# The RWKV-7 outputs of a hybrid two-layer model: one 64x64 inverse per chunk, outputs of two chunks beside the second solve, and low parts on GpSimd

## The chip, the cores and the metric

The kernel runs on one core of a Trainium2 chip. The metric is the time of one launch on the device, in microseconds (us); less is better. TensorE (PE in the rows) multiplies, VectorE (DVE), ScalarE (ACT) and GpSimd (POOL) do elementwise work, and SyncE (SP) issues the transfers.

## The reference

512 tokens of width 1024 pass two layers in float32. Layer 0 mixes with RWKV-7 (8 heads of 64) and gated linear attention (GLA, 4 heads), layer 1 with differential attention; a SwiGLU block of hidden width 2816 follows each. The change touches the mixer of layer 0 alone. Its RWKV part runs, for each head, over the tokens

```
def step(S, inp):
    r_t, w_t, k_t, v_t, a_t, b_t = inp
    sa = einsum('bhvk,bhk->bhv', S, a_t)
    S = S * w_t[:, :, None, :] + sa[..., None] * b_t[:, :, None, :] + v_t[..., None] * k_t[:, :, None, :]
    return S, einsum('bhvk,bhk->bhv', S, r_t)
...
y = rwkv7_recurrence(rh, heads(decay), kh, vh, -kk, kk * heads(a))
y = ((y - mean) * rsqrt(var + 64e-5)).reshape(Bsz, T, 512) * ln_w + ln_b
bonus = sum(rh * kh * r_k, axis=-1, keepdims=True) * vh
o_a = (y + bonus) * g                    # g = sigmoid(xg @ g1) @ g2
o_b = rms(gla(...)) * gla_norm * silu(gg)
return concatenate([o_a, o_b], axis=-1) @ w_out
```

## The kernel before

The matrices are transposed: channels lie on the 128 partitions, the 512 tokens along the free dimension. A projection (`form_a`) splits each weight block in a high part (`whi`, ScalarE, L96) and a low part (`wlo`, VectorE, L97) and issues three fast matmuls per 128x128 block (`mm3`, L107 to L109); other products are plain float32, and the trace shows two matmul records for each of them.

The recurrence runs in blocks of 64 tokens. A chunk `c` here is 128 channels, that is two heads, with all 8 blocks of tokens; there are four. `Chunk` makes the inputs of one (`key`, `receptance`, `value`) and the Gram products (`gram`): per head and block a unit lower triangular 64x64 matrix whose inverse is needed. `solve` inverts its 32x32 diagonal blocks for two chunks at once: 31 steps of a multiplication (`tmp`, L633) and an addition (`xl`, L635), framed by 32x32 transposes (L624, L638). The first solve (chunks 0, 1) runs on GpSimd during chunks 2 and 3, the second (chunks 2, 3) on VectorE.

`rwkv_out` forms a chunk's output. It applies the 64x64 inverse by three rounds of 128x128 products: the diagonal inverse (`z`, L661), the block below the diagonal (L668, added on VectorE as `w`, L670) and the diagonal inverse again (L675). Then come the state products (L697, L709), six state steps in series (L718, L719), the read-out (L728, L734), the group norm (L744 to L759), the bonus (L760) and the output gate (product L753 and L754, factor L761). A generator yields between the stages, and `interleave(gens, 5)` writes the four chunks with a lag of five stages.

The order on each engine comes from a planner: it places every instruction by the written order and modelled times, and the hardware keeps that order. `gla_gates` (24 matmuls for each of four heads, `gg`) is written ahead of the second solve and uses the first set of PSUM banks; the outputs use the second set, which takes the same banks. Behind the outputs the output projection runs in two halves: GLA's (`part`, into `pd` banks) and RWKV's (`ohi`, `olo`, into `o` banks).

Of the kernel before, what the change touches and what calls it, by code (L numbers as in the profile page):

```python
# [16 lines left out]
P = 128  # L17
T = 512
# [428 lines left out]

def gla_gates(g, pool, ob):
    nc = g.nc
    for h in range(4):  # L450
        pg = dbank(g)
        form_a(g, pg, g.ap["win"][16 + h], g.xhi, g.xlo)
        gg = pool.tile([P, T], F32, name="gg", bufs=2)
        nc.vector.tensor_mul(gg, pg, g.rstd)
        nc.scalar.activation(gg, gg, AF.Silu)
        o = pool.tile([P, T], F32, name="o", bufs=2)
        nc.sync.dma_start(o, ob[h])
        nc.gpsimd.tensor_mul(o, o, gg)
        nc.sync.dma_start(ob[h], o)


class Chunk:
# [74 lines left out]
    def receptance(self):  # L537
# [7 lines left out]
        nc.vector.scalar_tensor_tensor(q4(r), q4(r), self.col("rw_r_k"), self.k, op0=ALU.mult, op1=ALU.mult)  # L545
        self.pbn = bank(g)
        nc.tensor.matmul(self.pbn, lhsT=m0.bones, rhs=r, start=True, stop=True)

    def value(self):
# [5 lines left out]
        for e in range(2):  # L555
            nc.vector.scalar_tensor_tensor(self.vs[:, :, 1 - e], qe(p)[:, :, e], self.col("mu_v"), qe(d)[:, :, e],
                                           op0=ALU.mult, op1=ALU.add)
        for e in range(2):
            nc.vector.tensor_mul(qe(d)[:, :, e], qe(self.pbn)[:, :, e], self.vs[:, :, 1 - e])
        nc.sync.dma_start(st.bon[c], d)  # L560

    def gram(self):
        g, m0, st, c = self.g, self.m0, self.st, self.c
        nc, ar, bk = g.nc, self.ar, self.bk
        for e in range(2):
# [49 lines left out]
def solve(g, st, sp, eng, cs):  # L615
# [3 lines left out]
    n = cs[0]  # L619
    xl = sp.tile([P, 32, 32], F32, name=f"xl{n}")  # L620
    nc.gpsimd.memset(xl, 0.0)
    nc.gpsimd.memset(xl.rearrange("p t i -> p (t i)")[:, 0::33], 1.0)
    al = sp.tile([P, 32, 32], F32, name=f"al{n}")
    nc.vector.transpose(al.rearrange("p t i -> p (t i)"), st.dg.rearrange("p a c i t -> p t (a c i)"))  # L624
# [3 lines left out]
    buf = sp.tile([P, 256], F32, name=f"tmp{n}")  # L628
    yield
    for s in range(31):  # L630
# [4 lines left out]
        eng.tensor_add(xl[:, s + 1:, 0:s + 1], xl[:, s + 1:, 0:s + 1], tmp)  # L635
    yield
# [10 lines left out]
def rwkv_out(g, m0, st, sp, c, zeros):  # L647
# [3 lines left out]
    no, G = zeros[c % 2]  # L651
    for e in range(2):
        rows = slice(64 * e, 64 * e + 32)
        nc.scalar.copy(no.rearrange("p (a i) x -> p a i x", a=2)[rows, :, :, 64 * e + 32:64 * e + 64],
                       st.n21[rows, :, c])
    x4 = lambda t: t.rearrange("p (u x) -> p u x", u=4)
    z, w = {}, {}
    for ih in range(2):
        pu = x4(bank(g, use))
        for i in range(4):  # L660
            nc.tensor.matmul(pu[:, i], lhsT=st.xd[:, ih, c, i], rhs=st.r[:, ih, c, i], start=True, stop=True)  # L661
        z[ih] = sp.tile([P, 4, P], F32, name="z", bufs=2)
        nc.scalar.copy(z[ih], pu)
    yield
    for ih in range(2):
        pw = x4(bank(g, use))
        for i in range(4):
            nc.tensor.matmul(pw[:, i], lhsT=no[:, 4 * ih + i], rhs=z[ih][:, i], start=True, stop=True)  # L668
        w[ih] = sp.tile([P, 4, P], F32, name="w", bufs=2)
        nc.vector.tensor_add(w[ih], pw, st.r[:, ih, c])  # L670
    yield
    for ih in range(2):
        pu = x4(bank(g, use))
        for i in range(4):
            nc.tensor.matmul(pu[:, i], lhsT=st.xd[:, ih, c, i], rhs=w[ih][:, i], start=True, stop=True)  # L675
# [636 lines left out]
```

## Time and profile before

| | |
|---|---|
| median of 3 runs | 1336.83 us (1335.76 to 1337.07) |
| profiled execution | 1336.43 us, its span 1334.6 us |
| TensorE busy | 1302.7 us, 98% of the span |
| VectorE, ScalarE, GpSimd busy | 701.3, 563.9, 216.3 us |
| mean granted TensorE clock | 0.992 |

The span is the profiled part of the execution; the 1.8 us between it and its time lie around it. Busy time counts an engine as busy while any of its instructions runs; matmuls overlap, so a row's mean duration is longer than the distance to the next one. The granted clock is a share of 2.4 GHz.

### The profile page before, as it was taken

The numbers are of one execution on the slowest core, as the hardware profiler recorded it, in microseconds if no ns is written. First come the engines' busy times: TensorE is split into PE (matmuls) and PEld (weight loads), VectorE is DVE, ScalarE is ACT, GpSimd is POOL, SyncE is SP. The second block draws the span as 40 slices with busy tenths as digits, with TensorE's granted clock in tenths as the row PEclk, the third lists the DMA queues.
The fourth block names the chain that finished last, engine by engine and source line by source line (L and its number), as shares of the span: only waits on it lengthen the run. The fifth ranks groups of instructions, "written<-read, shape, count | busy, mean of one in ns | idle before, by whom it ended". The sixth has DMA issues, their size and how long they took to land.

```text
span 1334.6 us, 17753 instructions
## 1 busy us (share of the span) xinstructions
PE 1302.7 (98%) x6856; PEld 1065.9 (80%) x6856; DVE 701.3 (53%) x1197; ACT 563.9 (42%) x957; POOL 216.3 (16%) x205
## 2 busy tenths in 40 slices
PE   8999989899999999999999999999999999999998
PEld 6788767687878888888888887887888888888886
DVE  7465778954554433334434258888643434433342
ACT  5555866353443222223334347777432322322232
POOL 3011084211511110011112001110201110011110
PEclk9999989899999999999999999999999999999999
DMA  6222222423645323433234332211333323553331
GB/s 196 66 64 87 72 72 87 156 72 108 233 140 163 95 77 97 115 104 99 75 88 125 96 95 64 52 46 46 110 102 102 93 75 97 148 127 98 101 100 63
DMA packets 52719, 133.72 MB, mean 100 GB/s; under 512 B 6067, under 2 KB 8499, under 8 KB 52636
## 3 DMA queue, kind: packets, MB, share of 16 engines
q1 hardware_dynamic: 51772, 131.43, 32.8%
q8 instruction: 54, 0.88, 0.3%
q10 hardware_dynamic: 864, 1.17, 0.2%
q14 instruction: 29, 0.24, 0.1%
HBM read 121.74 MB, written 11.36 MB: 100 GB/s over the span
## 4 chain that ended last, share of the span: by engine, by line
PE 90%; DVE 7%; ACT 2%; issue 1%; DMA 0%; DVEq 0%; ACTq 0%
PE pd L109 24%; PE pd L108 24%; PE pd L107 24%; PE po L1054 2%; DVE wlo L97 1%; DVE tmp L633 1%; DVE xl L635 1%; PE sc L1029 1%; PE sc L1030 1%; PE o L109 1%; PE o L108 1%; PE o L107 1%; PE pt L1050 0%; PE o L675 0%; PE po L108 0%
## 5 line engine op out<-in xcount | busy, mean ns | idle before, releaser
L96 ACT CAST whi<-wraw 128x1024 fp32r<-128x1024 f32 (+2 forms) x240 | 210.4, 879 | 521.1 <-PE pd L108 302.0
L109 PE MATMUL pd<-xhi,wlo 128*128 128x512 f32 x1032 | 406.6, 394 | 0.0
L107 PE MATMUL pd<-xhi,whi 128*128 128x512 f32 x1032 | 405.6, 393 | 0.9 <-ACT xhi L188 0.9
L108 PE MATMUL pd<-xlo,whi 128*128 128x512 f32 x1032 | 405.8, 393 | 0.0
L97 DVE TENSOR_TENSOR wlo<-wraw,whi 128x1024 fp32r<-128x1024 f32 (+2 forms) x240 | 252.4, 1054 | 137.1 <-ACT whi L96 136.2
L107 PEld LDWEIGHTS pd<-xhi,whi 128*128 128x128 f32 x1032 | 193.8, 188 | 42.1 <-ACT xhi L188 1.3
L108 PEld LDWEIGHTS pd<-xlo,whi 128*128 128x128 f32 x1032 | 193.8, 188 | 41.1 <-issue 0.2
L109 PEld LDWEIGHTS pd<-xhi,wlo 128*128 128x128 f32 x1032 | 193.9, 188 | 40.4
L231 POOL TENSOR_TENSOR hlo<-h,hhi 128x512 fp32r<-128x512 f32 x44 | 67.3, 1529 | 546.3 <-ACT hhi L230 546.3
L227 DVE TENSOR_TENSOR ut<-pd,rstd 128x512 f32<-128x512 f32 x44 | 30.4, 692 | 146.3 <-PE pd L109 146.3
L107 PE MATMUL pd<-hhi,whi 128*128 128x512 f32 x264 | 102.7, 389 | 0.0
L108 PE MATMUL pd<-hlo,whi 128*128 128x512 f32 x264 | 102.7, 389 | 0.0
L109 PE MATMUL pd<-hhi,wlo 128*128 128x512 f32 x264 | 102.7, 389 | 0.0
L224 DVE TENSOR_TENSOR gt<-pd,rstd 128x512 f32<-128x512 f32 x44 | 30.4, 692 | 123.5 <-PE pd L109 121.4
L108 PEld LDWEIGHTS pd<-hlo,whi 128*128 128x128 f32 x264 | 49.6, 188 | 10.3
L107 PEld LDWEIGHTS pd<-hhi,whi 128*128 128x128 f32 x264 | 49.5, 188 | 10.3
L109 PEld LDWEIGHTS pd<-hhi,wlo 128*128 128x128 f32 x264 | 49.5, 188 | 10.3
L1034 ACT ACTIVATE s<-s,mn 128x384 f32<-128x384 f32 (+3 forms) x64 | 35.7, 559 | 21.4 <-DVE mn L1031 20.8
L230 ACT CAST hhi<-h 128x512 fp32r<-128x512 f32 x44 | 27.4, 622 | 35.5 <-DVE h L229 35.5
L240 DVE TENSOR_TENSOR xT<-pd,xT 128x512 f32<-128x512 f32 x24 | 16.6, 692 | 46.2 <-PE pd L109 46.2
L1010 POOL TENSOR_TENSOR qst<-q,qst 64x512 fp32r<-64x512 f32 x8 | 13.2, 1646 | 167.9 <-DVE qst L1008 167.9
L157 POOL TENSOR_TENSOR ssum<-nsq,ssum 128x512 f32<-128x512 f32 x21 | 31.5, 1498 | 49.9 <-ACT nsq L153 49.4
(384 smaller groups left out, 1837.4 us busy)
## 6 DMA issues: line engine op xcount, KB each, us to landing
wraw<-in_gate SPq DMA_DIRECT2D x44, 512.0 KB, 3.7
wraw<-in_up SPq DMA_DIRECT2D x44, 512.0 KB, 3.6
wraw<-in_win SPq DMA_DIRECT2D x40, 256.0 KB, 2.7
wraw<-in_down SPq DMA_DIRECT2D x24, 384.0 KB, 3.1
wraw<-in_wqk SPq DMA_DIRECT2D x16, 512.0 KB, 3.6
wraw<-in_down SPq DMA_DIRECT2D x24, 320.0 KB, 2.8
wraw<-in_downt SPq DMA_DIRECT2D x10, 512.0 KB, 3.7
xT<-in_xT SPq DMA_DIRECT2D x16, 256.0 KB, 3.9
```

Source lines behind the costliest of these rows:

```text
L96: nc.scalar.copy(hi, raw)
L97: nc.vector.tensor_sub(lo, raw, hi.bitcast(F32))
L107: nc.tensor.matmul(out, lhsT=lhi, rhs=rhi, start=start, stop=False)
L108: nc.tensor.matmul(out, lhsT=lhi, rhs=rlo, start=False, stop=False)
L109: nc.tensor.matmul(out, lhsT=llo, rhs=rhi, start=False, stop=stop)
L157: (nc.vector if c in fast else nc.gpsimd).tensor_add(ss, sq, first if c == 1 else ss)
L224: nc.vector.tensor_mul(gt, pg, rstd)
L227: nc.vector.tensor_mul(ut, pu, rstd)
L230: nc.scalar.copy(hhi[:, n], h)
L231: nc.gpsimd.tensor_sub(hlo[:, n], h, hhi[:, n].bitcast(F32))
L1034: nc.scalar.activation(s[:, m, :L], s[:, m, :L], AF.Exp, bias=mn[:, m:m + 1], scale=-1.0, accum_out=sm[:, m:m + 1])
L1054: nc.tensor.matmul(po[:, qb * P:qb * P + P], lhsT=att[:, b * P:b * P + P], rhs=v[:, b, h * P:h * P + P], start=b == 0, stop=b == qb)
```

## The change

- `below` forms the block below the diagonal of each 64x64 inverse once, by two rounds of 32x32 products, into `xd`; the three rounds of `rwkv_out` become one, on `st.r`, and L652 to L671 go. The solve also transposes its result into `xu` for that.
- The second solve yields every two steps and is interleaved with the outputs of chunks 0 and 1, without lag; `gla_gates` is written behind them and uses the second set of PSUM banks. The outputs of chunks 2 and 3 follow. The solves share `xl` and `tmp`.
- The output gate's product moves behind GLA as split matmuls (`rwkv_gate`), called right behind `gla`; it is stored in DRAM and loaded as `gt`. The stores and loads of `sg`, `tail`, `g2` and `tailw` for the outputs go.
- The bonus product (L545 to L547, L558 to L560) moves from `receptance` and `value` into `bonus`, which `gram` calls first.
- The low parts of the weights of `gla_gates` and of GLA's half of the output projection are made on GpSimd (`g.low`). GLA's outputs `o` stay in SBUF instead of going to DRAM and back a second time; all eight blocks go into a second `xhi`, `xlo`.

```diff
@@ split
-    nc.vector.tensor_sub(lo, raw, hi.bitcast(F32))
+    g.low.tensor_sub(lo, raw, hi.bitcast(F32))
@@ rwkv_gate
+def rwkv_gate(g, gp, st, sg, tail, tailw):
+    nc = g.nc
+    g2 = gp.tile([P, 512], F32, name="g2", bufs=1)
+    nc.sync.dma_start(g2, g.ap["g2"])
+    parts = []
+    for n, x in (("a", g2), ("b", sg), ("c", tailw[0:32]), ("d", tail[0:32])):
+        hi = gp.tile([P, T], F32R, name=n + "hi", bufs=1)[:x.shape[0]]
+        lo = gp.tile([P, T], F32R, name=n + "lo", bufs=1)[:x.shape[0]]
+        nc.scalar.copy(hi, x)
+        nc.vector.tensor_sub(lo, x, hi.bitcast(F32))
+        parts += [hi, lo]
+    for c in range(RC):
+        s = slice(c * P, c * P + P)
+        pg = dbank(g)
+        mm3(nc, pg, parts[0][:, s], parts[1][:, s], parts[2], parts[3], True, False)
+        mm3(nc, pg, parts[4][:, s], parts[5][:, s], parts[6], parts[7], False, True)
+        t = gp.tile([P, T], F32, name="gt")
+        nc.scalar.copy(t, pg)
+        nc.sync.dma_start(st.gate[c], t)
@@ gla_gates
+    os = []
     for h in range(4):
+        o = pool.tile([P, T], F32, name="o", bufs=4)
+        nc.sync.dma_start(o, ob[h])
+        os.append(o)
+    for h, o in enumerate(os):
         pg = dbank(g)
+        g.low = nc.gpsimd
         form_a(g, pg, g.ap["win"][16 + h], g.xhi, g.xlo)
+        g.low = nc.vector
...
         nc.gpsimd.tensor_mul(o, o, gg)
-        nc.sync.dma_start(ob[h], o)
+    return os
@@ Chunk
+    def bonus(self):
+        g, m0, st, c, r, d = self.g, self.m0, self.st, self.c, self.rk, self.vd
+        nc = g.nc
+        qe = lambda t: t.rearrange("p (m e t) -> p m e t", e=2, t=CH)
+        nc.vector.scalar_tensor_tensor(q4(r), q4(r), self.col("rw_r_k"), self.k, op0=ALU.mult, op1=ALU.mult)
+        pb = bank(g)
+        nc.tensor.matmul(pb, lhsT=m0.bones, rhs=r, start=True, stop=True)
...
@@ solve
+        if s % per == per - 1:
+            yield
...
+    xu = st.xp.tile([P, 32, 32], F32, name="xu", bufs=1)
+    nc.vector.transpose(xu.rearrange("p i u -> p (i u)"), xl.rearrange("p t i -> p i t"))
+    st.xu = xu.rearrange("p t (a c i) -> p t a c i", a=2, c=RC)
@@ below
+def below(g, st, sp, c):
+    nc = g.nc
+    pys = [bank(g, f"o{c % 2}")[:, 0:256].rearrange("p (a i f) -> p a i f", a=2, i=4) for _ in range(2)]
+    ya = sp.tile([P, 2, 4, 32], F32, name="ya", tag="H", bufs=2)
+    for a in range(2):
+        for i in range(4):
+            for e in range(2):
+                top, low = slice(64 * e, 64 * e + 32), slice(64 * e + 32, 64 * e + 64)
+                nc.tensor.matmul(pys[0][low, a, i], lhsT=st.n21[top, a, c, i], rhs=st.xu[top, :, a, c, i],
+                                 start=True, stop=True)
+    for e in range(2):
+        low = slice(64 * e + 32, 64 * e + 64)
+        nc.scalar.copy(ya[low], pys[0][low])
+    for a in range(2):
+        for i in range(4):
+            for e in range(2):
+                top, low = slice(64 * e, 64 * e + 32), slice(64 * e + 32, 64 * e + 64)
+                nc.tensor.matmul(pys[1][top, a, i], lhsT=ya[low, a, i], rhs=st.xd[low, a, c, i, low],
+                                 start=True, stop=True)
+    for e in range(2):
+        top, low = slice(64 * e, 64 * e + 32), slice(64 * e + 32, 64 * e + 64)
+        (nc.scalar.copy, nc.vector.tensor_copy)[e](st.xd[top, :, c, :, low], pys[1][top])
@@ rwkv_out
+    below(g, st, sp, c)
+    yield
...
-            nc.tensor.matmul(pu[:, i], lhsT=st.xd[:, ih, c, i], rhs=w[ih][:, i], start=True, stop=True)
+            nc.tensor.matmul(pu[:, i], lhsT=st.xd[:, ih, c, i], rhs=st.r[:, ih, c, i], start=True, stop=True)
...
-    pg = bank(g, use)
-    s = slice(c * P, c * P + P)
-    nc.tensor.matmul(pg, lhsT=st.g2[:, s], rhs=st.sg, start=True, stop=False)
-    nc.tensor.matmul(pg, lhsT=st.tailw[0:32, s], rhs=st.tail[0:32], start=False, stop=True)
+    gt = sp.tile([P, T], F32, name="gt", bufs=1)
+    nc.sync.dma_start(gt, st.gate[c])
...
-    nc.vector.tensor_mul(y, y, pg)
+    nc.vector.tensor_mul(y, y, gt)
@@ mixer0
-        with tc.tile_pool(name="gates", bufs=1, side="right") as sp:
-            gla_gates(g, sp, ob)
-        second = solve(g, st, slv, nc.vector, (2, 3))
+        second = solve(g, st, slv, nc.vector, (2, 3), 2)
         next(second)
-        for x in (first, second):
-            for _ in x:
-                pass
...
         psums.close()
         with ExitStack() as right:
             psum_pool(g, right, "ps1", o0=3, o1=2, pd=3)
...
-            interleave([rwkv_out(g, m0, st, sp, c, zeros) for c in range(RC)], 5)
...
+            for _ in first:
+                pass
...
+            def take(c):
+                nc.scalar.copy(g.xhi[:, c], ys[c])
+                nc.gpsimd.tensor_sub(g.xlo[:, c], ys[c], g.xhi[:, c].bitcast(F32))
+            interleave([second, out(0), out(1)], 0)
+            with tc.tile_pool(name="gates", bufs=1, side="right") as gt:
+                os = gla_gates(g, gt, ob)
+                next_acts(g)
+                for c in range(2):
+                    take(c)
+                for h, o in enumerate(os):
+                    nc.scalar.copy(g.xhi[:, 4 + h], o)
+                    nc.vector.tensor_sub(g.xlo[:, 4 + h], o, g.xhi[:, 4 + h].bitcast(F32))
+            interleave([out(2), out(3)], 5)
+            for c in range(2, 4):
+                take(c)
...
             for j in range(KD):
                 pd = dbank(g)
-                form_a(g, pd, ap["wout"][j][:, 512:], ghi, glo)
+                g.low = nc.gpsimd
+                form_a(g, pd, ap["wout"][j][:, 512:], g.xhi[:, 4:], g.xlo[:, 4:])
+                g.low = nc.vector
...
-                form_a(g, pd, ap["wout"][j][:, :512], st.ohi, st.olo)
+                form_a(g, pd, ap["wout"][j][:, :512], g.xhi, g.xlo)
```

## Rows read from the trace of the kernel before

**Rows 1.** The page, part 2: busy tenths in 40 slices of the span.

```profile
PE   8999989899999999999999999999999999999998
...
PEclk9999989899999999999999999999999999999999
```

**Rows 2.** The waits of TensorE, 0 to 370 us: total, times, longest.

```profile
PE o L661 <- DVE gg L454: 5.8, 1, 5.8
PE pb L547 <- DVE r L545: 4.5, 2, 3.6
```

**Rows 3.** Busy time by stretch: us, length, busy (instructions) by engine, clock, DMA, GB/s.

```profile
226.00:250.30 24.30, 18.52 (x81) 14.64 (x79) 22.44 (x49) 12.15 (x19) 3.91 (x3) 0.99 0.37 120
250.30:272.00 21.70, 18.70 (x195) 17.54 (x196) 19.84 (x47) 12.16 (x25) 5.41 (x5) 0.81 0.37 119
272.00:335.00 63.00, 62.71 (x786) 50.70 (x786) 29.85 (x72) 24.90 (x51) 8.59 (x7) 0.99 0.34 102
...
96.00:113.00 17.00, 17.00 (x126) 14.55 (x126) 4.41 (x10) 8.99 (x17) 0.00 (x0) 1.00 0.16 60
```

**Rows 4.** Timeline around the second solve: start, duration, engine, line, operation, [idle before].

```profile
224.49 2.00 DVE L624 STREAM_TRANSPOSE al<-dg 128x1024 f32<-128x1024 f32 x1 [1.37 <-ACT dg L608]
...
244.41 1.31 POOL L458 TENSOR_TENSOR o<-o,gg 128x512 f32<-128x512 f32 x1 [5.11 <-ACT gg L455]
244.50 1.49 DVE L633 TENSOR_TENSOR tmp<-al,xl 128x252 f32<-128x252 f32 x1
...
246.03 0.42 DVE L635 TENSOR_TENSOR xl<-xl,tmp 128x252 f32<-128x252 f32 x1
...
250.34 6.73 PE L661 MATMUL o<-r,ga 128*128 128x128 f32 x32 [5.81 <-DVE gg L454]
...
264.60 1.25 DVE L638 STREAM_TRANSPOSE dg<-xl 128x1024 f32<-128x1024 f32 x1
...
265.88 3.83 ACT L644 COPY ga<-dg 32x256 f32<-32x256 f32 x6 [0.80 <-DVE dg L638]
```

**Rows 5.** The chain that ended last: start, duration, engine, tile, line, records.

```profile
142.20 1.07 PE pb L597 x30
...
283.62 0.96 PE o L753 x2
284.58 1.05 PE o L754 x2
286.00 1.84 PE o L668 x16
```

**Rows 6.** Groups by line and shape, PE, 218 to 370: busy us, mean ns, idle.

```profile
L597 PE MATMUL pb<-xT,ga 64*64 64x64 f32 x32 | 1.5, 223 | 0.4 <-ACT xT L589 0.4
```

**Rows 7.** One tile, ohi: duration ns min/median/max, first and last start.

```profile
L107 PE MATMUL o<-ohi,whi x32: 393/395/397, 345.7 to 367.4; 128*128 128x512 f32 x32
```

**Rows 8.** Timeline of TensorE in the third chunk.

```profile
186.47 2.04 PE L547 MATMUL pb<-r,bones 128*128 128x512 f32 x2 [3.63 <-DVE r L545]
```

**Rows 9.** Groups by line, DVE, 226 to 266.5 us: busy us, mean ns, idle.

```profile
L635 DVE TENSOR_TENSOR xl<-xl,tmp 128x31 f32<-128x31 f32 (+15 forms) x31 | 12.6, 407 | 0.8
L633 DVE TENSOR_TENSOR tmp<-al,xl 128x31 f32<-128x31 f32 (+15 forms) x31 | 12.3, 398 | 0.8
L97 DVE TENSOR_TENSOR wlo<-wraw,whi 128x512 fp32r<-128x512 f32 x7 | 5.5, 785 | 0.9 <-ACT whi L96 0.9
...
L670 DVE TENSOR_TENSOR w<-o,r 128x512 f32<-128x512 f32 x2 | 1.4, 688 | 0.0
```

**Rows 10.** Groups by line, DVE, 266.5 to 336 us: busy us, mean ns, idle.

```profile
L719 DVE TENSOR_TENSOR S<-o,H 128x64 f32<-128x64 f32 x24 | 5.4, 223 | 16.1 <-PE o L718 15.9
```

**Rows 11.** Timeline at the end of the mixer's outputs.

```profile
309.26 1.05 PE L675 MATMUL o<-w,ga 128*128 128x128 f32 x8
...
324.08 0.62 ACT L762 CAST ohi<-y 128x512 fp32r<-128x512 f32 x1
...
334.94 0.62 ACT L762 CAST ohi<-y 128x512 fp32r<-128x512 f32 x1
```

More of the change, by code (lines that the diff above doesn't have):

```diff
@@ L564, in gram @@
         nc, ar, bk = g.nc, self.ar, self.bk
+        self.bonus()
         for e in range(2):
@@ L649, in rwkv_out @@
+def rwkv_out(g, m0, st, sp, c, G):
     nc = g.nc
     use = f"o{c % 2}"
[L651 to L657, printed above, removed]
+    below(g, st, sp, c)
+    yield
     for ih in range(2):
-        pu = x4(bank(g, use))
+        pu = bank(g, use).rearrange("p (u x) -> p u x", u=4)
@@ L660, in rwkv_out @@
         for i in range(4):
             nc.tensor.matmul(pu[:, i], lhsT=st.xd[:, ih, c, i], rhs=st.r[:, ih, c, i], start=True, stop=True)
[L662 to L670, printed above, removed]
@@ L823, in mixer0 @@
         ob, part = dram("ob", 4, P, T), dram("part", KD, P, T)
-        st.rt, st.bon, sgd, taild = dram("rt", RC, P, T), dram("bon", RC, P, T), dram("sg", P, T), dram("tail", 32, T)
+        st.rt, st.bon, st.gate = dram("rt", RC, P, T), dram("bon", RC, P, T), dram("gate", RC, P, T)
         with tc.tile_pool(name="gla", bufs=2) as gp:
@@ L833, in mixer0 @@
             m0.th, sg, tail = lora(g, rp, gp)
-            nc.sync.dma_start(sgd, sg)
-            nc.sync.dma_start(taild, tail[0:32])
             gla(g, m0, gp, v, tail, tailw, ob)
+            rwkv_gate(g, gp, st, sg, tail, tailw)
         st.fv = g.xT.rearrange("p k t -> p (k t)").rearrange(
@@ L847, in mixer0 @@
         st.wc = pp.tile([P, RC, NQ], F32, name="wc")
-        nos = [pp.tile([P, 8, P], F32, name=f"no{i}") for i in range(2)]
-        for t in nos:
-            nc.gpsimd.memset(t, 0.0)
-        left = ExitStack()
-        slv = left.enter_context(tc.tile_pool(name="solve", bufs=1))
+        slv = ctx.enter_context(tc.tile_pool(name="solve", bufs=1))
         st.dg = slv.tile([P, 2, RC, 4, 32], F32, name="dg")
@@ L902, in mixer0 @@
-            st.ohi = xo.tile([P, RC, T], F32R, name="ohi")
-            st.olo = xo.tile([P, RC, T], F32R, name="olo")
-            interleave([rwkv_out(g, m0, st, sp, c, zeros) for c in range(RC)], 5)
-            for h in range(4):
-                o = sp.tile([P, T], F32, name="o", tag="part", bufs=2)
-                nc.sync.dma_start(o, ob[h])
-                nc.scalar.copy(ghi[:, h], o)
-                nc.vector.tensor_sub(glo[:, h], o, ghi[:, h].bitcast(F32))
+            Gs = []
+            for i in range(2):
+                Gs.append(sp.tile([P, NQ, P], F32, name=f"G{i}"))
+                nc.gpsimd.memset(Gs[i], 0.0)
@@ new lines, in mixer0, with out @@
+            st.xp = sp
+            for _ in first:
+                pass
+            ys = {}
+            def out(c):
+                for y in rwkv_out(g, m0, st, sp, c, Gs[c % 2]):
+                    if y is not None:
+                        ys[c] = y
+                    else:
+                        yield
+            def take(c):
+                nc.scalar.copy(g.xhi[:, c], ys[c])
+                nc.gpsimd.tensor_sub(g.xlo[:, c], ys[c], g.xhi[:, c].bitcast(F32))
+            interleave([second, out(0), out(1)], 0)
@@ L910, in mixer0 @@
+            sp = right.enter_context(tc.tile_pool(name="late", bufs=2, side="right"))
             for j in range(KD):
                 pd = dbank(g)
-                form_a(g, pd, ap["wout"][j][:, 512:], ghi, glo)
-                t = sp.tile([P, T], F32, name="part", bufs=2)
+                g.low = nc.gpsimd
+                form_a(g, pd, ap["wout"][j][:, 512:], g.xhi[:, 4:], g.xlo[:, 4:])
+                g.low = nc.vector
+                t = sp.tile([P, T], F32, name="part")
                 nc.scalar.copy(t, pd)
@@ L1184, in build @@
         g = setup(ctx, tc, ap, dbg)
-        g.cols, g.ahead = cols, 0
+        g.cols, g.ahead, g.low = cols, 0, g.nc.vector
         if "mix0" in parts:
```

59 lines of the change are left out of this document (17 added, 42 removed).

## The prediction

> **What bounds the kernel now.** I read the page first. TensorE is busy in nearly every slice; the two weak places are slices 5 to 8, the recurrent mixer [rows 1]. Everything from the first feed-forward block on is untouched by the diff, so I looked only at the mixer, 0 to 368 us. The waits of TensorE there name two places that the diff touches: 5.8 us for the last `gg` of the gates, and 4.5 us (3.6 in one piece) for the product `r*r_k*k` [rows 2]. The stretches say the same: from 226 to 272 us TensorE is busy 18.5 of 24.3 us and 18.7 of 21.7, the second at a granted clock of 0.81; from 272 to 335 it is busy 62.7 of 63 us at 0.99 [rows 3]. So there are two regimes. Around the second solve VectorE sets the pace (22.4 of 24.3 us busy, 19.8 of 21.7); behind it TensorE does.
>
> The timeline shows why. The second solve's operand is transposed at 224.5 and its result at 264.6 to 265.85, on VectorE without a real gap; only then come six ScalarE copies (3.8 us) and the outputs of chunks 2 and 3 [rows 4]. The output matmuls of chunks 0 and 1 start at 250.3 after 5.8 us of idleness, since their PSUM banks belong to the pool that the gates still use; these 32 records take 6.73 us, where 16 of the same shape take 1.84 later [rows 4, 5]. That is half speed: after the pause the clock stood at its lower level, 1.2 GHz, which is how the stretch comes to 0.81.
>
> **The change, part by part.** All sums are against the profiled execution (1336.43 us, span 1334.6), 0.4 us under the median of the three runs.
>
> *One inverse instead of three products.* Each chunk had three rounds of eight 128x128x128 products; 16 records take 1.84 us [rows 5]. Two rounds go: −3.7 us a chunk. `below` adds two rounds of 16 products of 32x32x32, 64 records. The trace has none of that size; the nearest is L597, 64x64 on two alternating tiles, 30 records in 1.07 us, 36 ns a record [rows 5]. From below: half of it, if 32 columns take half the time of 64, 1.1 us a chunk. From above: each record waits for the one before, at its own mean duration of 223 ns [rows 6], 14.3 us a chunk. I take 36 ns, 2.3 us a chunk, because L597 alternates two tiles exactly as `below` does.
>
> The Trainium skill, page "TensorEngine Tiling (Array Packing)", section Key Properties, says that a change of the tiling mode drains the array, which speaks against 32-row products in a stream of 128-row ones. L597 already includes a change from and to 128-row matmuls, so the row says that it is cheap; if each of the 16 entries paid one undrained duration more (0.22 − 0.04 us), the sum would be some 3 us higher.
>
> *The output gate.* L753 and L754 go from each output, 0.96 + 1.05 us [rows 5]: −2.0 us a chunk. In their place come 24 split matmuls behind the gated linear attention. Split matmuls follow each other at 0.233 us (32 groups of three between 345.7 and 367.4) [rows 7], so +5.6 us, and there is nothing to hide them: TensorE is busy 17 of 17 us in 96 to 113 [rows 3]. Their eight casts and subtractions and four PSUM copies lie on ScalarE and VectorE, which are busy 9.0 and 4.4 of those 17 us: no cost while that cover lasts. The four stores and four loads of `gate` replace the stores and loads of `sg`, `tail`, `g2`, `tailw` and the second trip of `ob` on SP; there are fewer transfers in all. The four gate stores delay the release of the attention's space, but TensorE is 5.6 us later there as well: nothing.
>
> *Bonus with the Gram products.* The 3.6 us wait at L547, and the 2.04 us that its two records then take at the low clock (L753, the same shape, 0.96) [rows 5, 8], lose their place. The Gram products behind it need the same late VectorE results, so most of the wait passes to them. Bounds 0 and −5 us; I take −2, nearer to nothing.
>
> *VectorE in the second solve.* From 224.5 to 265.85 it ran 41.4 us. Out go seven low parts, 5.5 us, and two `w` additions, 1.4 us [rows 9]. In comes `xu`, a transpose like `al`, 2.0 us [rows 4]. In come the VectorE steps of the outputs of chunks 0 and 1: 272 to 335 holds four chunks' worth in 29.85 us [rows 3], so 7.5 each, +15 us. And the seven low parts on GpSimd hit the solve: while GpSimd multiplied for 1.31 us, a solve step took 1.49 instead of 0.42 us [rows 4], 1.05 lost; seven times, +7.4. Together 41.4 − 5.5 − 1.4 + 2.0 + 15 + 7.4 = 58.9, and the second solve ends at 283.4 instead of 265.85. From below: no collision, and the last third of the output steps after the solve (−12): 271. From above: VectorE also waits in order for the state steps, 16.1 us for four chunks [rows 10], 8 for two: 291.
>
> The Trainium skill, page "GPSIMD Engine Reference", section Engine selection, advises VectorE for elementwise work with two inputs, GpSimd being about twice as slow. The trace agrees (1.31 us against 0.69 for a VectorE operation of that shape [rows 4, 9]), and by the slowness alone the move would free VectorE, the solve ending 7.4 us earlier; the collision is what the row adds, and the sum goes by the row.
>
> *What then sets the end.* Freed banks let gates and outputs 0 and 1 run together from about 230 us, so the 5.8 us wait goes and VectorE is late next. After the solve: copies 3.8; `below` 4.2 (2.3 of matmuls, and three copies of 0.64 in series, the duration of one of the six); then from the third product to the written output as in chunk 3, 309.26 to 335.56, 26.3 [rows 11]; the second chunk later by half of the 10.9 us between the last two outputs (bounds 0 and 10.9) [rows 11], 5.5; then the output projection's second half, 22.5 [rows 7]. 283.4 + 3.8 + 4.2 + 26.3 + 5.5 + 22.5 = 345.7, against 368.2: −22.5. Its first half (22.4 us of matmuls) fills that chain.
>
> TensorE alone says nearly the same: 4 × (−3.7 − 2.0 + 2.3) = −13.6, and the idleness of 226 to 272, 24.3 − 18.5 + 21.7 − 18.7 = 8.8, and the slow 32 records, 6.73 − 3.7 = 3.0: −25.4.
>
> Sum: −22.5 + 5.6 − 2 = −18.9, 1336.4 − 18.9 = **1317.5 us**.
>
> **Rivals.**
> A, TensorE alone sets the end: VectorE collides little, the solve ends near 271, the rest is hidden. 1336.4 − 25.4 + 5.6 − 2 = 1314.6, with all 5 us of the bonus 1311.6, with `below` at half price 1307. For it: the solve's gaps are small, and 22 us of projection matmuls can fill. Against it: seven GpSimd operations do land in the solve.
>
> B, the overlap is weak: `bon`, `gt` and the shared `rb` buffer are single, so outputs 0 and 1, started in step, wait for each other, and VectorE stands in order behind them; the solve ends at 291 and the last chunk follows by 10.9. End 345.7 + 8 + 5.4 = 359, −9, plus 5.6, no gain from the bonus: 1333. For it: 16.1 us of VectorE's time already goes into waiting for state steps [rows 10]. SP is a second queue here: a load of `bon` for the next chunk waits for the buffer, with weight loads behind it. Against it: the solve's steps come first in the written order and need no other engine.
>
> C, slower: `below` is not pipelined. At 223 ns a record [rows 6] it costs 4 × 64 × 0.187 = 48 us more than I took and stands on the path of both pairs: 1365. It decides from 0.11 us a record on, where 256 × 0.074 eats the 18.9. Against it: L597 at 36 ns.
>
> **How the numbers follow.** The forecast gets 0.48, A 0.22, B 0.18, C 0.06; 0.06 stays for a mixer that stands about where it was because late VectorE leaves TensorE idle in the second pair, with the clock falling each time. About 0.2% (2.7 us) is what a measurement here can tell from no change; B at 1333 is just outside. Faster 0.86, same 0.05, slower 0.09. The range goes from A at half price (1306) to near B (1330); the forecast's own is 1309 to 1324.
>
> **What would show it.** Right: no product of 128x128 between `z` and `w`, no wait at the outputs for `gg`; solve steps of over 1 us beside GpSimd subtractions; the second solve's last transpose around 270 to 291; the mixer's last matmul near 349 (345.7 + 5.6 − 2); gate matmuls, 5.6 us, before the first chunk; `below` at some 36 ns a record. Wrong: TensorE idle more than 10 us between the second solve and the last output, or a wait for a low part on GpSimd ahead of gate or projection matmuls, or 32x32 records spaced over 0.1 us.

## The result, and the profile after

The changed kernel takes 1344.2 us (median of 6 runs, 1339.5 to 1345.8), the kernel before 1336.2 beside it: ratio 1.0051, 95% interval 1.0039 to 1.0063, half a per cent slower (some 7 to 8 us). The forecast was 1317.5, so 26.7 us are to be explained. The profiled execution has a span of 1343.1 us. Its page, part 2, answers to [rows 1]:

```profile
PE   8999997898999999999999999999999999999998
...
PEclk9998998898999999999999999999999999999999
```

Slices 4 (by its clock), 7 and 10 are weaker than they were; slice 6 is better. The waits of TensorE, 90 to 380 us, answer to [rows 2]:

```profile
PE pb L593 <- DVE r L591: 7.9, 2, 5.9
PE pd L107 <- ACT xhi L949: 4.6, 1, 4.6
```

The 5.8 us for `gg` are gone, as forecast. At the bonus product (L593 now) the wait of 3.6 us in chunk 2 has shrunk to 2.0, and a new one of 5.9 stands in chunk 3. The projection waits 4.6 us for the attention's output. Cut at the same four events (the `al` transposes of both solves, the second solve's `dg` transpose at its end, the last matmul of the mixer), the stretches of the kernel before are, with the columns of [rows 3]:

```profile
90.00:164.90 74.90, 73.67 (x537) 59.09 (x536) 47.09 (x102) 49.75 (x86) 5.40 (x10) 1.00 0.22 71
164.90:224.50 59.60, 54.18 (x322) 41.39 (x322) 48.02 (x80) 34.88 (x62) 45.10 (x66) 0.94 0.26 81
224.50:265.90 41.40, 35.48 (x291) 30.83 (x287) 38.69 (x84) 19.36 (x35) 9.27 (x9) 0.92 0.42 139
265.90:368.20 102.30, 99.15 (x943) 79.86 (x941) 52.16 (x103) 45.33 (x84) 28.10 (x21) 0.98 0.42 135
```

and those of the changed kernel:

```profile
90.00:178.70 88.70, 87.77 (x549) 66.68 (x549) 49.49 (x107) 51.86 (x89) 2.58 (x5) 0.94 0.25 84
178.70:244.00 65.30, 54.25 (x354) 40.92 (x349) 49.56 (x75) 33.69 (x58) 51.52 (x74) 0.92 0.24 73
244.00:296.60 52.60, 48.24 (x626) 40.04 (x623) 47.01 (x108) 24.97 (x46) 15.58 (x14) 0.94 0.25 78
296.60:376.20 79.60, 72.71 (x717) 58.62 (x715) 40.10 (x68) 40.83 (x76) 36.14 (x26) 0.96 0.49 160
```

Busy time times granted clock is roughly TensorE's work at full speed. Summed over the four stretches it falls from 254.4 to 247.6 us, −6.8 (forecast: 4 × −3.4 + 5.6 = −8.0). But the time in which TensorE idles grows from 15.7 to 23.2 us, and what it loses by running at a lower clock from 8.1 to 15.4. −6.8 + 7.5 + 7.3 = +8.0, which is what the mixer's end moves. So the work left about as forecast; idleness and clock, which in the forecast's sum for TensorE alone should have given 8.8 + 3.0 = 11.8 back, took 14.8. This is bookkeeping: it says where time went, not why. It is also coarse, since the clock has two digits: in windows of 1 us the clock loss is 7.3 before and 13.7 after, and the work falls by about 6.

| event, us | before | forecast | after |
|---|---|---|---|
| `al`, first solve | 164.9 | 170.5 | 178.7 |
| `al`, second solve | 224.5 | 228.1 | 244.0 |
| second solve ends | 265.9 | 287.0 | 296.6 |
| last output written | 335.6 | 326.8 | 345.3 |
| mixer ends | 368.2 | 349.3 | 376.2 |

Behind the forecast the stretches lose +8.2, +7.7, −6.3, +8.9 and +8.4 us.

**In front.** From 101.5 to 111.5 us the granted clock is 0.50, the lower level of 1.2 GHz, though TensorE never idles. Windows of the changed kernel:

```profile
97.00:101.50 4.50, 4.50 (x24) 2.90 (x21) 0.18 (x1) 4.27 (x7) 0.00 (x0) 1.00 0.02 4
101.50:111.50 10.00, 10.00 (x39) 8.36 (x38) 1.56 (x3) 1.33 (x3) 0.00 (x0) 0.50 0.34 131
```

Its timeline has there, between the attention's own products, the new gate products; those of the tail use 32 of the 128 rows:

```profile
99.71 0.50 PE L107 MATMUL pd<-bhi,ahi 128*128 128x512 f32 x1
...
100.60 0.50 PE L107 MATMUL pd<-dhi,chi 32*128 32x512 f32 x1
...
101.18 0.39 PE L109 MATMUL pd<-dhi,clo 32*128 32x512 f32 x1
101.50 0.80 PE L107 MATMUL pd<-bhi,ahi 128*128 128x512 f32 x1
102.09 1.05 PE L443 MATMUL pb<-ident,rn 128*128 128x128 f32 x4
102.94 1.71 PE L437 MATMUL pb<-dv,sq 128*128 128x1 f32 x8
```

The kernel before has 128-row projection matmuls in this place, at a clock of 1.00 [rows 3]. Even ahead of the fall, at the full clock, the products that alternate between 128 and 32 rows are dearer than the forecast's 0.233 us: three take 0.89 us from 99.71 and 0.90 from 100.60, where the forecast has 0.70.

**Chunk 3.** GpSimd makes the gates' low parts beside VectorE's chain. VectorE and GpSimd in the timeline after:

```profile
227.95 1.53 DVE L557 TENSOR_TENSOR gr<-gr,a 128x512 f32<-128x512 f32 x1 [0.16 <-ACT a L556]
229.52 2.77 DVE L562 TENSOR_TENSOR bkt<-gr,en 128x256 f32<-128x256 f32 x2
...
227.42 4.59 POOL L97 TENSOR_TENSOR wlo<-wraw,whi 128x512 fp32r<-128x512 f32 x3
```

The two operations of L562 together took 0.74 us in the kernel before (line 534 there):

```profile
215.27 0.74 DVE L534 TENSOR_TENSOR bkt<-gr,en 128x256 f32<-128x256 f32 x2
```

GpSimd's operations suffer too, 4.59 us for three. TensorE waits for the end of this chain:

```profile
234.32 2.04 PE L593 MATMUL pb<-r,bones 128*128 128x512 f32 x2 [5.87 <-DVE r L591]
```

In the kernel before, part of the gates' projection filled chunk 3's waits (by count some 18 of its 96 matmuls, 4 us); now it stands behind the outputs of chunks 0 and 1.

**Behind the second solve.** From 296.6 to 306.2 us TensorE is busy 3.16 of 9.60 us; windows, and the timeline, of after:

```profile
296.60:306.20 9.60, 3.16 (x70) 2.43 (x68) 4.28 (x7) 7.73 (x14) 5.00 (x5) 0.83 0.31 104
```

```profile
299.61 1.99 PE L699 MATMUL o<-xu,n 32*32 32x32 f32 x64 [1.88 <-DVE xu L686]
...
301.20 1.27 POOL L97 TENSOR_TENSOR wlo<-wraw,whi 128x512 fp32r<-128x512 f32 x1 [7.22 <-ACT whi L96]
302.43 1.27 POOL L486 TENSOR_TENSOR o<-o,gg 128x512 f32<-128x512 f32 x1
303.64 1.27 POOL L97 TENSOR_TENSOR wlo<-wraw,whi 128x512 fp32r<-128x512 f32 x1
...
306.09 1.29 POOL L486 TENSOR_TENSOR o<-o,gg 128x512 f32<-128x512 f32 x1
...
306.16 1.65 PE L107 MATMUL pd<-xhi,whi 128*128 128x512 f32 x3 [4.56 <-ACT xhi L949]
...
308.06 0.76 ACT L703 COPY ya<-o 32x256 f32<-32x256 f32 x2
```

The products `o*gg` alternate with low parts on GpSimd, the projection waits for their casts, and ScalarE comes to the `ya` copy of chunks 2 and 3, ready since 301.6, only behind those casts. One more cause stands here that the list of the change does not name: `gg` has one buffer where it had two, and VectorE waits 3.6 us for the product that reads it:

```profile
303.72 0.69 DVE L484 TENSOR_TENSOR gg<-pd,rstd 128x512 f32<-128x512 f32 x1 [3.59 <-POOL o L486]
```

What this buffer costs by itself was not run.

### The profile page after: what moved, and what is told of

Read it like the earlier page. It is cut to its first block, busy times and chain, and to the rows that moved or that the text cites. A ratio compares the mean times of both kernels' runs of the same rounds, so it can differ in the third digit from the quotient of the medians.

```text
span 1343.1 us, 18005 instructions
## 1 busy us (share of the span) xinstructions
PE 1303.4 (97%) x6992; PEld 1060.4 (79%) x6992; DVE 703.3 (52%) x1183; ACT 567.7 (42%) x963; POOL 235.6 (18%) x219
## 4 chain that ended last, share of the span: by engine, by line
PE 75%; DVE 4%; ACT 2%; issue 1%; POOL 0%; ACTq 0%; POOLq 0%; DVEq 0%
PE pd L107 21%; PE pd L108 21%; PE pd L109 21%; PE po L1101 1%; PE sc L1076 1%; PE sc L1077 1%; PE o L109 1%; PE o L108 1%; PE o L107 1%; DVE tmp L671 1%; PE po L107 0%; PE po L109 0%; PE po L108 0%; PE pt L1097 0%; PE o L767 0%
## 5 line engine op out<-in xcount | busy, mean ns | idle before, releaser
L107 PE MATMUL pd<-xhi,whi 128*128 128x512 f32 x1064 | 421.7, 397 | 5.4 <-ACT xhi L949 4.6
L108 PE MATMUL pd<-xlo,whi 128*128 128x512 f32 x1064 | 421.4, 396 | 0.2 <-DVE xlo L950 0.2
L109 PE MATMUL pd<-xhi,wlo 128*128 128x512 f32 x1064 | 421.5, 396 | 0.0
L97 DVE TENSOR_TENSOR wlo<-wraw,whi 128x1024 fp32r<-128x1024 f32 (+2 forms) x224 | 241.7, 1080 | 135.1 <-ACT whi L96 134.3
L107 PEld LDWEIGHTS pd<-xhi,whi 128*128 128x128 f32 x1064 | 200.9, 189 | 51.6 <-ACT xhi L949 4.7
L109 PEld LDWEIGHTS pd<-xhi,wlo 128*128 128x128 f32 x1064 | 201.0, 189 | 43.8 <-issue 2.3
L108 PEld LDWEIGHTS pd<-xlo,whi 128*128 128x128 f32 x1064 | 200.8, 189 | 43.8 <-DVE xlo L950 1.7
L108 PEld LDWEIGHTS pd<-hlo,whi 128*128 128x128 f32 x264 | 49.6, 188 | 10.2
```

The costliest lines, as they stand in the source:

```text
L97: g.low.tensor_sub(lo, raw, hi.bitcast(F32))
L107: nc.tensor.matmul(out, lhsT=lhi, rhs=rhi, start=start, stop=False)
L108: nc.tensor.matmul(out, lhsT=lhi, rhs=rlo, start=False, stop=False)
L109: nc.tensor.matmul(out, lhsT=llo, rhs=rhi, start=False, stop=stop)
```

## The experiments

Ratios to the kernel before, with 95% intervals; each kernel computes the whole reference.

| run | us | ratio |
|---|---|---|
| low parts on VectorE | 1339.5 | 1.0017 (1.0004 to 1.0029) |
| gate product back | 1347.1 | 1.0078 (1.0063 to 1.0093) |
| bonus back | 1352.8 | 1.0121 (1.0106 to 1.0136) |
| inverse alone | 1358.3 | 1.0163 (1.0146 to 1.0179) |
| gate operands filled up | 1341.7 | 1.0037 (1.0026 to 1.0049) |
| gate back, low on VectorE | 1348.1 | 1.0085 (1.0068 to 1.0103) |
| inverse alone, `xu` late | 1341.0 | 1.0029 (1.0019 to 1.0038) |
| no overlap | 1348.1 | 1.0077 (1.0055 to 1.0098) |
| gates in front | 1343.7 | 1.0055 (1.0040 to 1.0070) |
| gates in front, gate back | 1345.9 | 1.0072 (1.0055 to 1.0088) |
| bonus alone | 1338.3 | 1.0010 (1.0000 to 1.0019) |
| gates in front, own `xl` | 1333.8 | 0.9984 (0.9967 to 1.0001) |
| **filled up, low on VectorE** | **1331.5** | **0.9961 (0.9946 to 0.9976)** |
| filled up, gates' low on VectorE | 1338.5 | 1.0014 (1.0003 to 1.0025) |
| filled up, low on VectorE, bonus back | 1338.9 | 1.0018 (1.0009 to 1.0028) |

**Low parts on VectorE.** In the changed kernel:

```diff
-        g.low = nc.gpsimd
+        g.low = nc.vector
```

> The changed kernel with all low parts on VectorE again. Theory 1 (GpSimd's low parts make VectorE late, in the fourth chunk and in the second solve, and hold up the last products of o and gg on GpSimd's own queue): the wait for the bonus product in the fourth chunk falls from 5.9 us to under 4, the wait for the cast of o (4.6 us) goes, and the time falls from 1344 to 1334 to 1338. Rival (VectorE is the bound there, so 16 low parts of 0.69 us = 11 us on it cost as much as the collisions): 1343 to 1348, second solve no shorter than 52 us.

Some 4.5 us faster, a little less than theory 1 said: the bonus wait in chunk 3 falls from 5.9 to 3.2 us, the wait for the cast of `o` from 4.6 to 1.7. The second solve's operand comes at 237.6 instead of 244.0, the end of the mixer 6.3 us earlier. Not all of this is GpSimd's: 2.1 us are already there at the first `al` (176.6 against 178.7), ahead of any low part on GpSimd, where the order of the instructions differs and the clock's fall in front came later and was shorter. The second solve became longer, 56.5 us against 52.6.

**Gate product back in the outputs.** In float32, its operands loaded into the free space of the first solve:

```diff
-            rwkv_gate(g, gp, st, sg, tail, tailw)
...
-    gt = sp.tile([P, T], F32, name="gt", bufs=1)
-    nc.sync.dma_start(gt, st.gate[c])
+    pg = bank(g, use)
+    nc.tensor.matmul(pg, lhsT=st.g2[:, s], rhs=st.sg, start=True, stop=False)
+    nc.tensor.matmul(pg, lhsT=st.tailw[0:32, s], rhs=st.tail[0:32], start=False, stop=True)
```

> The changed kernel with the output gate's product back in the outputs, in plain float32 (its operands in the space of the first solve's transposed matrix). Theory 2 (the gate's matmuls behind the linear attention cost 5.6 us and the clock drop from 101 to 112 us, another 5.3): the clock stays at 1.0 there, the first chunk's key step comes at 117 instead of 128 us, and with 8 us more products in the outputs the time is 1339 to 1342. Rival (the clock falls there anyway, from the small products of the linear attention): key step at 122, time 1344 to 1348.

The clock in front stays at 1.00 and the first `al` comes at 164.5, as before the change; but chunks 2 and 3 then take 74.2 us. The waits of SyncE's queue, 160 to 245 us, show why:

```profile
SPq L934 <- POOL xl L675: 21.1, 1, 21.1
SPq L931 <- POOL tmp L673: 18.1, 1, 18.1
```

Two loads into the first solve's space wait for GpSimd, with chunk 3's weights behind them. That is this edit's own fault, so neither theory is tested by the time, and this run and its sibling below price nothing.

**Bonus back.**

```diff
-        self.rk = r
+        nc.vector.scalar_tensor_tensor(q4(r), q4(r), self.col("rw_r_k"), self.k, op0=ALU.mult, op1=ALU.mult)
+        self.pbn = bank(g)
+        nc.tensor.matmul(self.pbn, lhsT=m0.bones, rhs=r, start=True, stop=True)
...
-        self.bonus()
```

> The changed kernel with the bonus product back in receptance and value. Theory 3 (the bonus in the Gram stage puts its VectorE product behind the value's and TensorE waits 5.9 us in the fourth chunk): that wait falls to 2 us or less and the time to 1338 to 1341. Rival (VectorE is late there for other reasons, GpSimd's low parts): the wait only moves, time 1343 to 1346.

8.6 us slower, where the theory expected a gain and the rival no change: both miss. TensorE waits 10.1 us at the product, and the mean granted clock is 0.980 against 0.986.

**The inverse alone**, in the kernel before: `below` and `xu`, one round of products.

```diff
+    xu = st.xus[cs[0] // 2]
+    nc.vector.transpose(xu.rearrange("p i u -> p (i u)"), xl.rearrange("p t i -> p i t"))
...
+    below(g, st, sp, c)
...
-            nc.tensor.matmul(pw[:, i], lhsT=no[:, 4 * ih + i], rhs=z[ih][:, i], start=True, stop=True)
```

> The kernel before with the single 64x64 inverse alone (below, one round of products, xu for each solve), all else as before. If TensorE's removed work counts in full, 4 x 3.4 = 13.6 us: 1322 to 1325. If the chain from the solve to the outputs counts, the copies and the transpose for it (4 us of VectorE, 4.2 us in series) eat part: 1327 to 1333. If the 32x32 products are not pipelined: 1340 or more.

The third expectation's time, by another cause, so not a price of the inverse either: the first solve's `xu` transpose came early in VectorE's order and waited 18.9 us for GpSimd, with chunk 2 behind it. TensorE's longest wait, 165 to 230 us:

```profile
PE pb L583 <- DVE gr L577: 21.1, 1, 21.1
```

**Gate operands filled up to 128 rows**, with zeros:

```diff
+        if k < P:
+            y = gp.tile([P, T], F32, name=n + "pad", bufs=1)
+            nc.gpsimd.memset(y, 0.0)
+            nc.vector.tensor_copy(y[0:k], x)
```

> The changed kernel, with the 32-row operands of the gate products filled up with zero rows to 128; the same number of matmuls. Theory: the fall of the granted clock to 0.50 between 101.5 and 111.5 us, with TensorE busy all the time, comes from the products that use 32 of the 128 rows, beside the attention's own narrow products. Then the clock stays near 1.0 there, the first chunk's key step starts some 5 us earlier than 128.2 us, and the kernel takes about 1339 us. Rival: the clock falls there for another reason than the rows (the order of the products, the 128x1 and 64x64 products alone): still 0.50 for some 10 us, and 1344 us.

Of the clock the theory holds. Windows and timeline of this run:

```profile
101.50:111.50 10.00, 10.00 (x91) 9.04 (x88) 2.16 (x5) 4.37 (x10) 0.00 (x0) 1.00 0.34 131
```

```profile
100.30 0.40 PE L107 MATMUL pd<-dhi,chi 128*128 128x512 f32 x1
...
101.00 0.40 PE L107 MATMUL pd<-bhi,ahi 128*128 128x512 f32 x1
```

The same number of matmuls, the clock stays at 1.00, and three products of the tail take 0.70 us where they took 0.90. The first `al` comes 5.9 us earlier. Half of that is lost again by the mixer's end (−3.0). The median, 2.5 us lower, lies between the two expectations, and the two intervals overlap, so in time this mend alone isn't clear of the noise.

The other traces bear out the clock. All four with the 32-row products in front have the fall, though not at one place or of one length: some 10 us in the changed kernel, 13.7 with the bonus back, 6.8 with the low parts on VectorE and as much without the overlap. All six with filled-up operands show 1.00 from 97 to 120 us. Low parts on VectorE:

```profile
100.00:110.00 10.00, 10.00 (x82) 8.19 (x81) 1.55 (x3) 3.44 (x7) 0.00 (x0) 1.00 0.34 131
110.00:120.00 10.00, 10.00 (x36) 7.20 (x37) 1.73 (x4) 2.24 (x6) 0.00 (x0) 0.66 0.21 81
```

The 128x1 and 64x64 products are in the filled-up versions too, so they alone don't bring the fall; whether 32 rows would without them wasn't run.

**Gate back, low parts on VectorE**: the two edits above together.

> The changed kernel with the gate product back in the outputs and the low parts back on VectorE. With the gate back alone the first solve's operand was ready at 164.5 us as in the kernel before, but chunks 2 and 3 then took 74.2 us up to the second solve's operand, against 59.6 before. Theory: GpSimd's low parts cause those 14.6 us, by collision with VectorE; without them the second solve's operand is ready near 226 us and the kernel takes 1328 to 1334 us. Rival: they come from the work that now shares TensorE and VectorE with chunks 2 and 3 (other fillers in the place of the gates' projection): the operand is still ready near 236 us or later, and the kernel takes 1340 us or more.

The operand came at 239.0, the rival's time, but the loads on SyncE's queue wait for the first solve again (21.1 us), which neither theory had: nothing is decided.

**The inverse alone, `xu` late**: both transposes issued when the outputs' space is open.

```diff
+            for i in range(2):
+                xu = sp.tile([P, 32, 32], F32, name=f"xu{i}")
+                nc.vector.transpose(xu.rearrange("p i u -> p (i u)"), st.xl[i].rearrange("p t i -> p i t"))
```

> The kernel before, with the single inverse alone (one round of products in place of three, and the 32x32 products), and the transposes of both solves issued only when the outputs' space is open, so that VectorE doesn't stop for the first solve on GpSimd, as it did for 19 us in the earlier run of this edit. Theory: the 32x32 products and the three PSUM copies in series put back what the two rounds of products gave, the more so at a lower granted clock: 1334 to 1341 us. Rival (the forecast's own sum): 4 x (3.7 - 2.3) = 5.6 us come off TensorE in the outputs, which it bounds: 1331 us or less.

The theory's time, though not by its reason: the second solve ends at 269.4 us, but the first `xu` ran at 257.6, late in the second solve, and TensorE waited 13.5 us for it where it had waited 5.8 for `gg`. The inverse without such a wait wasn't run alone.

**No overlap**, low parts on VectorE:

```diff
-            interleave([second, out(0), out(1)], 0)
...
+            for _ in second:
+                pass
+            interleave([out(c) for c in range(RC)], 5)
```

> The changed kernel with its low parts on VectorE and without the overlap: the gates first, then the second solve to its end, then the outputs of all four chunks as in the kernel before. Theory: the overlap does gain, some 8 to 12 us between the second solve's operand and the mixer's end (132 us against 144 before); without it 1347 to 1352 us. Rival: the overlap costs, as the outputs' steps delay the second solve (52.6 against 41.4 us) and the gates start late: 1330 to 1337 us.

The overlap gains 0.6%, some 8 us (1.0077 against 1.0017): the theory holds.

**Gates in front** of the second solve, low parts on VectorE, operands filled up.

```diff
+        with tc.tile_pool(name="gates", bufs=1, side="right") as sp:
+            gla_gates(g, sp, ob)
         second = solve(g, st, slv, nc.vector, (2, 3), 2)
...
-                os = gla_gates(g, gt, ob)
```

> The changed kernel with its low parts on VectorE, the gate operands filled up to 128 rows, and the gates of the attention where the kernel before has them: between chunk 3 and the second solve, with the attention's output back through HBM. Theory: in the changed kernel nothing is left to fill TensorE's waits in chunk 3 (5.9 us for the product of bones, 11.1 us idle in chunks 2 and 3 against 5.4) since the gates wait for the second solve's outputs; with them in front chunk 3 is covered, the second solve's operand is ready at some 230 us, and the kernel takes 1326 to 1333 us, less than the kernel before. Rival: the gates keep their banks and the outputs of chunks 0 and 1 start only near 255 us, the solve is half over by then and the overlap is lost: 1338 us or more.

The time lies in the rival's range, but neither reason holds. Chunk 3 is covered (3.5 us of idleness in chunks 2 and 3) and the second operand comes at 231.1. But its solve begins at 260.7, since both solves share one `xl`, and its memset on GpSimd waits for the first one's late `xu`:

```profile
256.57 2.02 DVE L686 STREAM_TRANSPOSE xu<-xl 128x1024 f32<-128x1024 f32 x1 [1.73 <-DMA ob<-o]
...
258.66 0.95 POOL L661 MEMSET xl<- 128x1024 f32 x1 [0.32 <-DVE xu L686]
...
260.75 0.21 DVE L671 TENSOR_TENSOR tmp<-al,xl 128x31 f32<-128x31 f32 x1 [1.57 <-POOL xl L662]
```

**Gates in front, gate back**, its loads in the outputs' own space.

```diff
+            st.g2, st.sg = sp.tile([P, 512], F32, name="g2"), sp.tile([P, T], F32, name="sg")
+            nc.sync.dma_start(st.g2, ap["g2"])
```

> As the run with the gates in front, but with the gate product in the outputs as in the kernel before, in float32, from operands that are loaded when the outputs' space is open (so that no load stands on SyncE's queue behind the first solve, as it did for 21 us in the two earlier runs with the gate product back). Theory: the gate product costs 24 matmuls, 5.6 us, in front and gives 2.0 us a chunk back where TensorE is the bound, 8 us: without it the second solve's operand is 5 to 6 us earlier, and the whole is the same as with it to 3 us. Rival: the outputs are not bound by TensorE's work, so the 8 us weren't given back: 4 us or more faster than with it.

2 us slower than with the gate product in front, with intervals that overlap: the two are the same within what can be told, as the theory said. The operand comes 5.5 us earlier (225.6) and the second solve ends 4.6 earlier; the longer outputs take that back. Both runs have the late start of the second solve, so this price holds for that arrangement only.

**Bonus alone**, in the kernel before: the edit of "bonus back", reversed.

> The kernel before with the bonus product moved to the Gram products, nothing else. Theory: in the kernel before the wait of 3.6 us in chunk 2 stands at the product of bones with projection matmuls queued behind it; moved, it goes, and the clock doesn't fall there (0.74 in 180 to 190 us): 1330 to 1333 us. Putting it back into the changed kernel cost 8.6 us. Rival: most of the wait passes to the Gram products, as the forecast had it: 1334 to 1337 us.

No gain: the rival, if anything 1 us more. TensorE's waits in chunk 2 get shorter and pass to the products behind. The clock does rise in chunks 2 and 3, from 0.94 to 1.00, as the theory said, but the stretch takes 60.3 us against 59.6 and the second solve, on VectorE, ends at 267.7 against 265.9: clock that TensorE gets back need not become time.

**Gates in front, own `xl`** (and `tmp`; `part` has one buffer, to make room).

```diff
-    xl = sp.tile([P, 32, 32], F32, name="xl")
+    xl = sp.tile([P, 32, 32], F32, name=f"xl{cs[0]}")
```

> As the run with the gates in front, but the second solve has its own buffers for the inverse and its products, as in the kernel before; in the change both solves share one, so that the second could begin only at 260.8 us there, after the late transpose of the first, though its operand was ready at 231.1. Theory: with its own buffer the second solve begins at 233 us and ends at 275 to 285 us, and the kernel takes 1328 to 1335 us. Rival: the solve's end isn't what sets the mixer's end, which moves by less than 4 us: 1339 us or more.

The second solve ends at 280.6, as the theory said, and the kernel is 10 us faster than with the shared buffer. The runs spread widely (1329 to 1341 us), and the interval holds 1: no gain over the kernel before is shown.

**Filled up, low parts on VectorE**: the changed kernel with these two mends.

> The changed kernel with the gate operands filled up to 128 rows and the low parts on VectorE, the two mends together. Each alone took the median down by 2.5 and 4.7 us. If the places are independent: 1337 us. If the time that the clock gives back in front is lost again in chunks 2 and 3 (as 3 of 6 us were with the filled-up operands alone): 1339 us or more.

Faster than either expectation, and than the kernel before, by 0.39% (four runs). Its four stretches:

```profile
90.00:171.50 81.50, 80.54 (x536) 62.01 (x537) 48.35 (x104) 51.80 (x88) 2.58 (x5) 1.00 0.26 91
171.50:232.40 60.90, 52.62 (x355) 40.17 (x349) 49.27 (x79) 33.66 (x58) 46.97 (x69) 0.97 0.24 79
232.40:287.40 55.00, 47.81 (x626) 40.29 (x623) 48.06 (x117) 27.24 (x50) 10.60 (x11) 0.97 0.29 92
287.40:362.60 75.20, 71.37 (x712) 58.57 (x712) 38.34 (x71) 38.40 (x71) 26.48 (x19) 0.95 0.48 156
```

Clock loss is 6.6 us instead of 15.4, idleness 20.3 instead of 23.2; the last output is written at 332.1, the mixer ends at 362.6.

Beside the run that was only filled up, this one prices the low parts, since nothing else differs:

| stretch, us | low on GpSimd | on VectorE |
|---|---|---|
| to the first `al` | 82.8 | 81.5 |
| chunks 2 and 3 | 66.2 | 60.9 |
| second solve | 51.5 | 55.0 |
| to the mixer's end | 82.6 | 75.2 |

Chunks 2 and 3 with the low parts on GpSimd:

```profile
172.80:239.00 66.20, 56.48 (x356) 43.34 (x350) 50.64 (x74) 33.70 (x58) 51.09 (x73) 0.90 0.22 73
```

In the solve itself GpSimd's low parts even gained 3.5 us; they lost 5.3 ahead of it and 7.4 behind it.

**Filled up, only the gates' low parts on VectorE.**

```diff
-        g.low = nc.gpsimd
         form_a(g, pg, g.ap["win"][16 + h], g.xhi, g.xlo)
```

> The changed kernel with the gate operands filled up to 128 rows, and only the gates' low parts back on VectorE; those of the projection's half stay on GpSimd. Theory: the low parts cost where they run in chunk 3 and the second solve, beside VectorE's own chain, so this is as fast as with all of them on VectorE, 1331 to 1333 us. Rival: the projection's low parts on GpSimd cost too, behind the second solve, where GpSimd also has the products o*gg and the outputs' low parts: 1336 us or more.

The rival: both places cost, 3.2 us of the median in the gates (against filled up alone) and 7.0 in the projection. Three of the projection's low parts run ahead of the solve's end, which comes 5 us later than with all on VectorE.

**Filled up, low parts on VectorE, bonus back**: the edits shown above.

> The version with both mends (gate operands filled up, low parts on VectorE, 1331.5 us) with the bonus product back in the receptance and value steps. In the changed kernel the bonus at its old place cost 8.6 us, in the kernel before its move gained nothing. Theory: at its old place the product stands ahead of projection matmuls in chunks 2 and 3, and the clock falls in each wait, which the change feels more since it has fewer matmuls to fill in: 1335 to 1340 us. Rival: the 8.6 us were mostly the clock's fall at the gate products, which grew from 5.1 to 8.5 us in that run and doesn't take place here: within 2 us of 1331.5.

7.4 us slower, with the clock at the gate products at 1.00: the theory's time, and the rival is out. The place is only half the theory's. In chunks 2 and 3 the wait at the product is 8.6 us against 5.2; but the first `al` already comes 5.4 us later (176.9), of 8.2 at the mixer's end, with TensorE idle for 3.2 us against 1.0 up to there.

## Why the prediction was wrong

**The gate, +5.6: mis-sized, and this failed first.** Work and place were right; the sum took 0.233 us a matmul as the price of any split matmul, from rows of 128-row operands [rows 7]. With 32-row operands the stretch from 101.5 us ran at 0.50, which costs 5.0 us (10.0 us at half speed), and groups of three took 0.90 us at the full clock where 0.70 was counted, some 1.6 us if all eight paid it; the forecast had weighed such changes of the row count for `below`, not here. The first `al` came 8.2 us behind the forecast; filled up and with the low parts on VectorE it comes 1.0 behind. The Trainium skill, page "TensorE: Matmul & The Clock Gate", section "HAM oscillation — how this bites in real kernels", looks for such falls in gaps where TensorE idles. This trace differs, 10.00 of 10.00 us busy, and the measurement decides. A forecast that looks for idleness alone cannot see such a fall.

**Low parts on GpSimd: priced in the wrong place.** The sum gave them 7.4 us inside the second solve, on the path to the end, for seven of them, and nothing elsewhere. Of the sixteen, six ran in the solve, four in chunk 3, and six after the solve on GpSimd's queue among the `o*gg`. The solve itself took 52.6 us, less than the 58.9 forecast, and with the low parts back on VectorE it is longer, not shorter (55.0 against 51.5): the term of 7.4 was wrong there, and what the move cost, 10.2 us of the median (1341.7 to 1331.5, operands filled up), came in chunk 3 and behind the solve. Together with the filled-up operands it holds 12.7 us (1344.2 to 1331.5); singly the two mends gave 2.5 and 4.7. That they add to more than their sum is measured, by 5.5 us with an uncertainty of some 3.5; that each loss brings waits in which the other grows is argued from the clock of the stretches only.

**"The 5.8 us wait goes and VectorE is late next": half true.** It went. But the gates whose banks caused it had also filled chunk 3, and that cover was not counted as lost: idleness of chunks 2 and 3 went from 5.4 to 11.1 us. Low parts on VectorE bring it to 8.3, and the gates in front as well to 3.5, so the cover was worth 4.8 of it. The forecast's −8.8 for idleness was therefore a trade, not a gain. In the whole it was an even one: with the gates in front and an own `xl` the kernel takes 1333.8 us against 1331.5 with the gates behind, the same within what can be told, and the wait for `gg` (5.8 us) is back.

**"Its first half fills that chain": failed by 8.4 us, the largest part that the two mends leave.** The gates, 22 us of matmuls themselves, moved into the same place; the projection could begin only at 306 us. It still had 8.3 us to do when the last output was written (345.3 to 353.6), and in the mended version as much. There the solve ends at 287.4, the forecast's 287.0; the chain to the last output is 4.9 us longer than forecast, this remainder 8.0, and the mixer ends 13.3 us behind. That the gates' move is why the first half was late is read from the order of the two; no run took the gates away from there and left the rest.

**What held.** `below` is pipelined: 64 records took 1.99 us, 31 ns a record against the 36 taken, and rival C is out. The overlap gains, some 8 us. The bonus moved alone gains nothing (ratio 1.0000 to 1.0019), nearer to the forecast's bound of 0 than to its −2; in the changed kernel the old place would cost 7 to 9 us more. The case that came is the one given 0.06: TensorE idle, the clock falling each time, the mixer later than before; its clock loss in front, without idleness, was in none.

**Open.** The single inverse was not priced by itself, as both runs of it alone brought a wait for `xu`. A version with gates in front, own buffers and the gate product back wasn't run. Why the chain from the solve to the last output is 4.9 us longer than forecast in the mended version stays open; TensorE waits 4.2 us there for the second `xu`, a transpose that the forecast put inside the solve.

## What to carry to other kernels

A matmul's price is its duration and what it does to the clock around it: where operands of few rows move into a stretch of narrow products, look at the granted clock there; zero rows are a cheap thing to try. When work is moved out of a waiting place, ask what it had covered; work that seems off the bound may be the filler of someone's wait. Before counting GpSimd as a free engine, list what VectorE runs at that minute, and what stands next on GpSimd's queue.

## What the runs showed of the hardware

The granted clock fell to 0.50 for 7 to 14 us with no idle gap in all four kernels with 32-row products among narrow ones, and 128 rows of which 96 are zero kept it at 1.00 in all six, at the same number of matmuls. Three 32-row matmuls between 128-row ones took 0.90 us at the full clock, filled up 0.70. Two VectorE operations with two inputs in SBUF took 2.77 us beside GpSimd's subtractions and 0.74 without; the Trainium skill, page "SBUF — State Buffer", section "SBUF: two separate sides", says that the two engines share a port pair which one of them holds for its whole operation. The trace agrees: 1.0 us lost by each, less than the 1.5 us that one of GpSimd's took there. Products of 32x32x32 on alternating tiles went at 31 ns a record.
